# Modulation sums spread over the stages by rates, their loads tied to a value that each stage makes; second expert table turned and the last norm taken token by token

## The chip, the cores and the metric

One NeuronCore of a Trainium2 chip runs the whole program; the other cores are idle. The metric is the device time of one execution in microseconds, as the median of several runs. Five engines work side by side, each through its own list of instructions in order: TensorE (PE, matmuls; its weight loads are shown as PEld), VectorE (DVE), ScalarE (ACT), GpSimd (POOL) and SyncE (SP, which here only issues DMAs). An instruction waits on semaphores for what it needs, and everything behind it on its engine waits with it. A DMA is issued from an engine's list, so an issue that has to wait holds up that engine too.

## What is computed

256 latent tokens and 256 context tokens, 1024 wide, go through two layers (l = 0 works on both, l = 1 on the latents alone), and then the latents through a second block. Cut to what matters:

```python
for l in range(2):                                    # block 1
    ml = split(silu(c) @ w_ada[l] + b_ada[l], 6)      # modulation vectors, latents
    mc = split(silu(c_ctx) @ w_ada[l] + b_ada[l], 6)  # the same for the context (l = 0)
    h = modulate(rmsnorm(x), ml[0], ml[1])
    y = mixer(h)      # 4 mLSTM heads, 8 differential attention heads, Fourier, merged by gates
    x = x + ml[2] * y
    x = x + ml[5] * swiglu(modulate(rmsnorm(x), ml[3], ml[4]))
# block 2: HGRN and S5 mixer, then PEER (128 x 128 = 16384 experts), modulated in the same way
x = x + gt2 * peer(h2)      # sum over experts: gates * gelu(h2 . u_e) * v_e
return rmsnorm(x, final_norm_w)
```

All in float32. A matmul of float32 exactness is made of three fp32r matmuls: high part by high part, high by low, low by high.

## The kernel before

**Tables.** Every weight table comes by DMA as a `raw` tile of 128 x 1024 (512 KB, three buffers). ACT casts it to the high part `whi` (L181, or L201 in the stretches whose order is written out), DVE subtracts to get the low part `wlo` (L186, L202); two buffers each. PE then runs the three products of each table. Activations have hi and lo tiles in the same way (`h`, `hl`, `yb`).

**Background work.** The program is written as a stream of table products; after each one `spend(us)` is called with its estimated time. `spend` advances a clock, and for each `step` of it calls `tick`, which lets the heads started with `go` (mLSTM, attention, Fourier) put their next few small instructions between the products. `spend` also calls `fill` once, which takes the next item of the list `todo`.

**Modulation.** `todo` holds the work on `w_ada`. Part of layer 0's is done on PE at the start (`ada_half`). The rest are 208 sums on DVE (L353, in `ada_sums`): a row tile `ada` of 128 x 1024 is multiplied by the activated conditioning vector `cb`, broadcast over the partitions, and added up along the row. The `ada` tiles are 128 loads of 512 KB into two buffers, issued from SP's queue, which also carries the weight tables. In layer 0 one load serves two sums (64 sums, latents and context); for layer 1 (96) and block 2 (48) it serves one. `ada_rows` makes `cb`: one load of 1 MB (later one of 0.5 MB), a tanh on ACT in pieces (L323) and a product on DVE (L325). Layer 0 needs its remaining vectors by the end of its mixer, layer 1 by its start, and so on.

**Who sets the order.** In the automatic stretches the build's scheduler orders each engine's list by what is ready; there the position in which the code states a sum or a load says little, unless something that the sum needs is made late. After `ordered()` (start and `first_products`, the FFN with `norm_ahead`, PEER) each engine keeps the order that is written.

**End.** `peer_v` walks over the 128 tables of the second expert table in pairs. The gates times activations are kept as hi and lo tiles (`pAh`, `pBl`, 256 tokens). The table is the weight that PE holds and the tokens stream by: 24 matmuls per table of 128 x 256 into four accumulators `ps`, `ps`, `po`, `pada`, with dimensions down the partitions. After the last pair come the residual (L2092), squares (L2094), their sums over partitions by small matmuls (L2084), the root (L416, L417), its spread over the partitions (L425), a copy (L2105), eight products (L2108, L2110) and eight stores (L2111). The output leaves the chip transposed, and the host turns it.

In the profile the functions are found at: `spend` L109, `ada_rows` L313, `ada_load` L328, `ada_sums` L334, the mLSTM heads' chains L772 to L851, attention L879 to L952, `peer_v` L2023.

Of the kernel before, what the change touches and what calls it, by code (L numbers as in the profile page):

```python
# [30 lines left out]
P = 128  # L31
# [8 lines left out]
STEP = [(4.4, 2.8, 3.2), (4.6, 3.3, 2.6)]  # L40
CTX, LAT = slice(0, T), slice(T, T2)
# [8 lines left out]
class K:  # L50
    def __init__(self, tc, d, ctx):
# [6 lines left out]
        self.todo = []  # L58
        self.ahead = []
# [253 lines left out]
    def ada_rows(self, src, ns):  # L313
# [3 lines left out]
        nc.sync.dma_start(cb, bass.AP(tensor=src.tensor, offset=src.offset, ap=[[0, P], [D, ns], [1, D]]))  # L317
# [399 lines left out]
    def ml_qkv(self, l, h, hs, need_ctx, qk):  # L717
# [6 lines left out]
        for i in range(0 if qk else 2):  # L724
            for t, w, c in ((k, "w_mlk", cols), (q, "w_mlq", qc)):
                acc = self.ps("acc")
                self.gemm_t(acc[:, c], d[w][l, 2 * h + i], hs, c)
                nc.scalar.copy(t[:, i, c], acc[:, c])  # L728
        self.tok_major(v, d["w_mlv"][l, h], hs, range(4))
        return q, k, v  # L730

    def tok_major(self, v, src, hs, tts):
# [4 lines left out]
        for i, a in enumerate(accs):  # L737
            nc.scalar.copy(v[:, tts[2 * i]:tts[2 * i] + 2].rearrange("p a b -> p (a b)"), a)

    def ml_o(self, l, h, hs, th):  # L740

        W = self.W
        for i in range(2):
            acc = self.ps("acc")
            self.gemm_t(acc[:, :W], self.d["w_mlo"][l, 2 * h + i], hs, self.hc)
            self.nc.scalar.activation(th[:, i, :W], acc[:, :W], AF.Tanh, scale=0.5)  # L746

# [134 lines left out]
    def da_qk(self, l, h, hs, need_ctx):  # L882
# [9 lines left out]
        nc.scalar.copy(k, acc)  # L892

# [89 lines left out]
    def merge(self, l, b, n, hs, ys, y):  # L983
# [4 lines left out]
        nc.scalar.activation(th[:, :W], acc[:, :W], AF.Tanh, scale=0.5)  # L988
        acc = self.ps("acc")
# [98 lines left out]
    def layer(self, l, x, ada, *begun):  # L1088
# [25 lines left out]
        if l == 0:  # L1114
# [3 lines left out]
            for i, acc in enumerate(accs[1:]):  # L1118
                nc.scalar.copy(qk[(i + 1) % 2][:, i // 2], acc)
        else:  # L1120
# [42 lines left out]
        self.step = STEP[l][0]  # L1163
# [8 lines left out]
        self.step = STEP[l][1]  # L1172
        for h in range(8):
# [5 lines left out]
            if h == 1:  # L1179
                self.drain("ml")  # L1180
                for n in range(KT):
                    self.merge(l, 0, n, hs, ys, y)
        streams_fn = [0, 1] if need_ctx else [1]
        self.step = STEP[l][2]
# [59 lines left out]
        self.ordered()  # L1244
        hs = []
# [777 lines left out]
    def peer_v(self, G, spill, sgs, x, ada, fw, out):  # L2023
# [40 lines left out]
        for j in range(P - 2):  # L2064
# [7 lines left out]
            for n in range(KT):  # L2072
                product(i, e, hi, lo, n, j == 0, False)

        w = [self.wload(d["peer_v"][:, 2 * pairs[63] + e], 8, P) for e in range(2)]
        sq, ss = G[:, 2 * KT:3 * KT], self.ps("t")

        def weighted(n):
            for m in (n - 1, n):
                nc.scalar.activation(G[:, m], x[m], AF.Copy, scale=fw[:, m:m + 1])  # L2080

        def sums(n):
            for j in range(2):
                nc.tensor.matmul(ss[:, j:j + 1], sq[:, n, j * P:(j + 1) * P], c["one1"], start=n == 1 and j == 0,  # L2084
                                 stop=n == KT - 1, skip_group_check=j == 1)

        for n in range(KT):
            for e in range(2):
                product(63, e, *w[e], n, False, e == 1)
            if n % 2:  # L2090
                for m in (n - 1, n):
                    nc.vector.scalar_tensor_tensor(x[m], accs[m // 2][:, (m % 2) * T:(m % 2) * T + T],  # L2092
# [228 lines left out]
```

## Time and profile before

| | |
|---|---|
| median of 3 runs | 3074.4 us (3071.04 to 3077.4) |
| profiled execution | 3075.71 us, of which the traced span is 3073.9 us |
| PE busy | 2961.0 us, 96% of the span |
| DVE busy | 2147.3 us, 70% |
| ACT busy | 1332.0 us, 43% |
| POOL busy | 408.0 us, 13% |
| mean granted TensorE clock | 0.988 of full speed |

The stretches are, by time in the span: start and first products to about 60 us; layer 0's mLSTM heads 60 to 300, attention to 700 (with the first merge, products of w_gp and of the branch table, between heads 1 and 2), last two merges 700 to 850, output product and FFN to 1200; layer 1's heads around 1250 to 1500, attention to 1750, its FFN to about 2000; block 2 to the end, with the two expert tables from about 2300 on. Busy PE means that a matmul stood in the array's pipeline, not that it worked at its peak; idle time of another engine costs nothing unless PE, or the end, waits for it.

### The profile page before, as it was taken

What the parts mean: (1) busy time and instruction counts of PE and PEld (TensorE: products, weight loads), DVE (VectorE), ACT (ScalarE), POOL (GpSimd) and SP (SyncE); (2) the same over time, 40 slices, a digit from 0 to 9 for tenths busy, and PEclk for the clock granted to TensorE, in tenths of its full rate; (3) what the DMA queues carried; (4) which work ended last, traced back from release to release, by engine and by line L of the source; (5) the groups of instructions that cost most, each with busy time, mean ns of one, the idle gap of its engine ahead of it and who ended that gap; (6) DMA issues with size and microseconds to landing.
All of it is one profiled execution on the core that took longest, in us unless ns stands there. A gap on an engine that the chain in (4) does not pass through costs nothing.

```text
span 3073.9 us, 51558 instructions
## 1 busy us (share of the span) xinstructions
PE 2961.0 (96%) x20266; PEld 2680.2 (87%) x20266; DVE 2147.3 (70%) x4042; ACT 1332.0 (43%) x2289; POOL 408.0 (13%) x493
## 2 busy tenths in 40 slices
PE   7999999999999999989999999999899999999998
PEld 5777787888887888878898999987899999999998
DVE  5998637754367555897668667688589878866665
ACT  3333425543243222443446554454445444544444
POOL 2211101101130000321001122770200000000000
PEclk9999999999999999999999999999999999999999
DMA  7555222112333343467442355542457765466664
GB/s 254 178 191 172 70 89 71 67 49 83 100 120 117 132 150 142 152 223 258 142 133 96 111 197 168 179 151 90 134 181 229 231 198 161 154 233 230 224 233 165
DMA packets 151283, 480.90 MB, mean 156 GB/s; under 512 B 19616, under 2 KB 23520, under 8 KB 150912
## 3 DMA queue, kind: packets, MB, share of 16 engines
q1 hardware_dynamic: 145584, 466.39, 46.0%
q0 software_dynamic: 2576, 7.55, 0.9%
q8 instruction: 159, 2.61, 0.4%
q10 hardware_dynamic: 2880, 3.67, 0.3%
q14 instruction: 84, 0.69, 0.1%
HBM read 459.42 MB, written 18.12 MB: 155 GB/s over the span
## 4 chain that ended last, share of the span: by engine, by line
issue 29%; PE 16%; DVE 6%; DMA 2%; ACT 1%; POOL 1%; POOLq 0%; DVEq 0%; ACTq 0%
PE pacc L235 4%; PE pacc L234 4%; PE pacc L233 4%; DMA ada<-in_w_ada_dram 2%; DVE wlo L186 1%; DVE junk L353 1%; PE pacc L231 1%; DVE wlo L202 1%; PE po L845 1%; PE pacc L253 0%; PE pacc L255 0%; PE pacc L254 0%; DVE ropeb L879 0%; POOL ssum L403 0%; DVE hl L506 0%
## 5 line engine op out<-in xcount | busy, mean ns | idle before, releaser
L186 DVE TENSOR_TENSOR wlo<-raw,whi 128x1024 fp32r<-128x1024 f32 x480 | 609.6, 1270 | 352.4 <-ACT whi L181 345.7
L181 ACT CAST whi<-raw 128x1024 fp32r<-128x1024 f32 x480 | 502.7, 1048 | 747.9 <-PE pacc L234 450.9
L233 PE MATMUL pacc<-h,whi 128*128 128x512 f32 (+1 forms) x1280 | 475.1, 371 | 2.0 <-ACT q L728 1.3
L235 PE MATMUL pacc<-h,wlo 128*128 128x512 f32 (+1 forms) x1280 | 467.3, 365 | 5.6 <-DVE wlo L186 5.6
L234 PE MATMUL pacc<-h,whi 128*128 128x512 f32 (+1 forms) x1280 | 467.4, 365 | 3.0 <-DVE h L506 3.0
L233 PE MATMUL pacc<-hl,whi 128*128 128x256 f32 x1504 | 430.1, 286 | 0.2 <-ACT whi L201 0.2
L234 PE MATMUL pacc<-hl,whi 128*128 128x256 f32 x1504 | 425.4, 283 | 4.7 <-DVE hl L506 4.4
L235 PE MATMUL pacc<-hl,wlo 128*128 128x256 f32 x1504 | 425.7, 283 | 3.2 <-DVE wlo L202 1.5
L201 ACT CAST whi<-raw 128x1024 fp32r<-128x1024 f32 (+2 forms) x207 | 189.9, 926 | 375.2 <-PE pacc L234 281.9
L234 PEld LDWEIGHTS pacc<-hl,whi 128*128 128x128 f32 x1504 | 286.4, 190 | 6.5 <-DVE hl L506 6.1
L235 PEld LDWEIGHTS pacc<-hl,wlo 128*128 128x128 f32 x1504 | 285.2, 190 | 4.6 <-DVE wlo L202 2.4
L233 PEld LDWEIGHTS pacc<-hl,whi 128*128 128x128 f32 x1504 | 287.1, 191 | 0.5 <-ACT whi L201 0.4
L235 PEld LDWEIGHTS pacc<-h,wlo 128*128 128x128 f32 x1280 | 243.2, 190 | 48.0 <-DVE wlo L186 7.7
L353 DVE SCALAR_TENSOR_TENSOR junk<-ada,cb 128x1024 bf16<-128x1024 f32 x208 | 258.3, 1242 | 35.7 <-DMA ada<-in_w_ada_dram 34.7
L234 PEld LDWEIGHTS pacc<-h,whi 128*128 128x128 f32 x1280 | 243.6, 190 | 44.0 <-DVE h L506 4.6
L233 PEld LDWEIGHTS pacc<-h,whi 128*128 128x128 f32 x1280 | 243.2, 190 | 44.2 <-ACT q L728 1.5
L202 DVE TENSOR_TENSOR wlo<-raw,whi 128x1024 fp32r<-128x1024 f32 (+2 forms) x163 | 200.2, 1228 | 96.4 <-ACT whi L201 95.7
L235 PE MATMUL pacc<-yb,wlo 128*128 128x512 f32 (+1 forms) x624 | 225.2, 361 | 0.8 <-DVE wlo L186 0.7
L233 PE MATMUL pacc<-yb,whi 128*128 128x512 f32 (+1 forms) x624 | 226.0, 362 | 0.0
L234 PE MATMUL pacc<-yb,whi 128*128 128x512 f32 (+1 forms) x624 | 224.9, 360 | 0.0
L253 PE MATMUL pacc<-whi,h 128*128 128x256 f32 x704 | 202.5, 288 | 3.2 <-ACT oth L746 3.2
L255 PE MATMUL pacc<-wlo,h 128*128 128x256 f32 x704 | 198.9, 283 | 4.9 <-DVE wlo L186 3.3
(587 smaller groups left out, 6480.9 us busy)
## 6 DMA issues: line engine op xcount, KB each, us to landing
ada<-in_w_ada_dram SPq DMA_DIRECT2D x128, 512.0 KB, 3.7
raw<-in_peer_u_dram SPq DMA_DIRECT2D x128, 512.0 KB, 3.8
raw<-in_peer_v_dram SPq DMA_DIRECT2D x128, 512.0 KB, 3.7
raw<-in_w_f_dram SPq DMA_DIRECT2D x120, 512.0 KB, 3.7
raw<-in_w_gp_dram SPq DMA_DIRECT2D x48, 512.0 KB, 3.3
spill<-k SPq DMA_DIRECT2D x61, 256.0 KB, 4.2
k<-spill SPq DMA_DIRECT2D x61, 256.0 KB, 2.6
raw<-in_w_out_dram SPq DMA_DIRECT2D x24, 512.0 KB, 3.3
```

What stands on the lines that cost most here:

```text
L181: nc.scalar.copy(hi, raw)
L186: self.nc.vector.tensor_sub(lo, raw, hi)
L201: self.nc.scalar.copy(hi, raw)
L202: (self.nc.gpsimd if self.spare else self.nc.vector).tensor_sub(lo, raw, hi)
L231: nc.tensor.matmul(acc, hi[:, k], xh[:, cols], start=k == first, stop=(k + 1) % kt == first)
L233: nc.tensor.matmul(acc, hi[:, k], xh[:, cols], start=k == first, stop=False)
L234: nc.tensor.matmul(acc, hi[:, k], xl[:, cols], start=False, stop=False)
L235: nc.tensor.matmul(acc, lo[:, k], xh[:, cols], start=False, stop=(k + 1) % kt == first)
L253: nc.tensor.matmul(a, xh[:, s], hi[:, k], start=half + k == 0 and not sk, stop=False, skip_group_check=sk)
L255: nc.tensor.matmul(a, xh[:, s], lo[:, k], start=False, stop=half * 4 + k == 7, skip_group_check=sk)
L353: nc.vector.scalar_tensor_tensor(self.junk, wt, 0.5, self.cb[:, s], op0=ALU.mult, op1=ALU.mult, accum_out=out[:, s, 8 * r + j:8 * r + j + 1])
L845: nc.tensor.matmul(po[:, :w], aT[:, s * P:(s + 1) * P], vof(s), start=s == 0, stop=s == nk // P - 1)
```

## The change

1. `spend` no longer takes one item of `todo` per product. It adds `us * rate` to `owed` and takes an item for each whole unit. `RATE` gives a rate for each layer and stage: heads, attention, the first merge, and the rest with the FFN.
2. The loads of `ada` and `cb` are issued from ACT's queue instead of SP's, and each is preceded by a copy on ACT of one element (`behind`) of a tile that the current stage has just made (`recent`) into the tile to be loaded. The load then can't come before that value is there. In the FFN `recent` is None and the order is the written one.
3. `wait`, the number of idle items before layer 0's first sums, goes from 4 to 1.
4. `peer_v` is turned: the gate tiles (128 tokens of `pAh` or `pBl`) are the weights that PE holds, and the table streams by in rows of 512, so that a table takes 12 matmuls of 128 x 512 and the accumulators have tokens down the partitions. Residual, gate vector and norm weight are brought to that form ahead (16 transposes of `x` on PE with 4 copies on ACT; four loads that spread a row over the partitions). The last two pairs are held to the end and run accumulator by accumulator, their parts in `pAh`/`whi` and `hl` tiles. Each accumulator's squares are summed along the row by ACT's accumulator, and the root, scaling and store (four of 256 KB) follow by token block.

```diff
+RATE = [(0.12, 0.03, 0.28, 0.30), (0.1, 0.1, 0.2, 0.0)]
...
     def spend(self, us):
-        self.fill()
+        self.owed += us * self.rate
+        while self.owed >= 1.0:
+            self.owed -= 1.0
+            self.fill()
...
         cb = self.t([P, 2, D], "cb", 1)[:, :ns]
-        nc.sync.dma_start(cb, bass.AP(tensor=src.tensor, offset=src.offset, ap=[[0, P], [D, ns], [1, D]]))
+        self.behind(cb[:, 0])
+        nc.scalar.dma_start(cb, bass.AP(tensor=src.tensor, offset=src.offset, ap=[[0, P], [D, ns], [1, D]]))
...
+    def behind(self, t):
+
+        if self.recent is not None:
+            self.nc.scalar.copy(t[0:1, 0:1], self.recent)
+
     def ada_load(self):
         if self.ada_src:
             wt = self.t([P, D], "ada", 2)
-            self.nc.sync.dma_start(wt, self.ada_src.pop(0))
+            self.behind(wt)
+            self.nc.scalar.dma_start(wt, self.ada_src.pop(0))
...
                 nc.scalar.copy(t[:, i, c], acc[:, c])
+                self.recent = t[0:1, i, c][:, 0:1]
...
-        self.step = STEP[l][0]
+        self.step, self.rate = STEP[l][0], RATE[l][0]
...
         self.ordered()
+        self.recent, self.rate = None, RATE[l][3]
...
-        def product(i, e, hi, lo, n, f, l):
-            wh, wl = ws[i]
-            o = accs[n // 2][:, (n % 2) * T:(n % 2) * T + T]
-
-            nc.tensor.matmul(o, hi[:, n], wh[:, e], start=f and n % 2 == 0, stop=False, skip_group_check=n % 2 == 1)
-            nc.tensor.matmul(o, hi[:, n], wl[:, e], start=False, stop=False, skip_group_check=n % 2 == 1)
-            nc.tensor.matmul(o, lo[:, n], wh[:, e], start=False, stop=l, skip_group_check=n % 2 == 1)
+        def product(i, e, hi, lo, a, f, l):
+
+            wh, wl = (w[:, e, a // 2 * P:a // 2 * P + P] for w in ws[i])
+            vh, vl = (v[a % 2] if isinstance(v, list) else v[:, a % 2 * 4:a % 2 * 4 + 4].rearrange("p a b -> p (a b)")
+                      for v in (hi, lo))
+            nc.tensor.matmul(accs[a], wh, vh, start=f, stop=False)
+            nc.tensor.matmul(accs[a], wl, vh, start=False, stop=False)
+            nc.tensor.matmul(accs[a], wh, vl, start=False, stop=l)
...
+        def transposed(a):
+            pt = self.ps("acc")
+            for j in range(4):
+                nc.tensor.transpose(pt[:, j * P:(j + 1) * P], x[a % 2 * 4 + j][:, a // 2 * P:a // 2 * P + P], c["ident"])
+            xt.append(take())
+            late.append((xt[-1], pt))
...
+        for a in range(4):
+            for i in (62, 63):
+                for e in range(2):
+                    product(i, e, *w[i, e], a, False, (i, e) == (63, 1))
+            x0, y = take(), take()
+            nc.vector.tensor_mul(x0, accs[a], gt[a % 2])
+            nc.vector.tensor_add(x0, x0, xt[a])
+            nc.scalar.activation(junk, x0, AF.Square, scale=1.0 / 32, accum_out=ss[:, a:a + 1])
+            nc.vector.tensor_mul(y, x0, fwr[a % 2])
+            ys.append(y)
+            if a % 2:
+                col = ss[:, 4 + a:5 + a]
+                nc.vector.scalar_tensor_tensor(col, ss[:, a - 1:a], 1e-6, ss[:, a:a + 1], op0=ALU.add, op1=ALU.add)
+                nc.gpsimd.tensor_tensor(rs[:, a:a + 1], col, c["mhalf"][:, 0:1], op=ALU.pow)
+                r = rs[:, a:a + 1]
+                nc.scalar.activation(ys[a - 1], ys[a - 1], AF.Copy, scale=r)
+                nc.scalar.dma_start(out[a // 2][:, 0:T2], ys[a - 1])
+                nc.vector.tensor_scalar(ys[a], ys[a], r, None, op0=ALU.mult)
+                nc.sync.dma_start(out[a // 2][:, T2:D], ys[a])
```

What the build makes of it is seen in the engines' lists. In ACT's list at the start of the program, where `h` are the high parts of the first normed activations (each serves `first_products` on PE), before:

```order
L201 CAST whi_414<-raw_259 128x1024
L504 ACTIVATE h_441<-k_105_438,ada_14_104 128x256 x2
L504 ACTIVATE h_450<-k_108_447,ada_14_104 128x256 x2
L201 CAST whi_456<-raw_306 128x1024
L504 ACTIVATE h_463<-k_113_460,ada_14_104 128x256 x2
L504 ACTIVATE h_472<-k_116_469,ada_14_104 128x256 x2
```

and now:

```order
L208 CAST whi_414<-raw_259 128x1024
L345 DMA ada_436<-in_w_ada_dram 128x1024
L345 DMA ada_438<-in_w_ada_dram 128x1024
L325 DMA cb_440<-in_c_rows_dram 128x2048
L518 ACTIVATE h_447<-k_108_444,ada_14_104 128x256 x2
L331 ACTIVATE pada_865<-cb_440 128x512
L518 ACTIVATE h_456<-k_111_453,ada_14_104 128x256 x2
L208 CAST whi_462<-raw_306 128x1024
L331 ACTIVATE pada_971<-cb_440 128x512
L518 ACTIVATE h_469<-k_116_466,ada_14_104 128x256 x2
```

Three loads and the tanh of `cb` (L331) now stand between the casts and the `h` of the first products; of the loads, that of `cb` waits for the semaphore that the first `ada` load signals when it has landed.

In DVE's list in layer 0's mLSTM heads, before, where `den` and `e` are a head's own chain and `junk` is a modulation sum:

```order
L353 SCALAR_TENSOR_TENSOR junk_101,ada_14_104<-ada_1820,cb_796 128x1024
L804 TENSOR_SCALAR e_192_917<-e_192_917,den_194_924 128x256
L796 TENSOR_TENSOR den_206_981<-den_206_981,gc_870 128x2
L186 TENSOR_TENSOR wlo_1072<-raw_1068,whi_1070 128x1024
L805 SCALAR_TENSOR_TENSOR e_192_917<-e_191_916,den_194_924,e_192_917 128x128
L797 RECIPROCAL den_206_981<-den_206_981 128x2
L353 SCALAR_TENSOR_TENSOR junk_101,ada_14_104<-ada_1916,cb_796 128x1024
L799 TENSOR_SCALAR e_196_933<-e_196_933,den_206_981 128x256
```

and now, around the same table:

```order
L812 SCALAR_TENSOR_TENSOR den_206_981<-den_978 128x2
L813 TENSOR_TENSOR den_206_981<-den_206_981,gc_872 128x2
L814 RECIPROCAL den_206_981<-den_206_981 128x2
L816 TENSOR_SCALAR e_196_933<-e_196_933,den_206_981 128x256
L817 SCALAR_TENSOR_TENSOR e_196_933<-e_197_934,den_206_981,e_196_933 128x128
L193 TENSOR_TENSOR wlo_1072<-raw_1068,whi_1070 128x1024
```

The sums between the links of the chain are gone from this place. By their place in the list between the same products, the 208 sums stood before 8 up to 100 us, 86 in 100 to 300, 66 in 925 to 1300 and 48 in 1300 to 1500; now they stand 4 up to 100, 10 in 100 to 300, 24 in 300 to 475, 21 in 575 to 700, 33 in 700 to 850, 87 in 925 to 1300, 10 in 1325 to 1500 and 19 in 1500 to 1750 (on the time scale of the kernel before).

Where they went is seen, for one, in DVE's list in layer 0's first merge (L1011 adds a merged product to the sum `x`), now:

```order
L193 TENSOR_TENSOR wlo_3427<-raw_3423,whi_3425 128x1024
L367 SCALAR_TENSOR_TENSOR junk_101,ada_14_104<-ada_3416,cb_440 128x1024
L1011 SCALAR_TENSOR_TENSOR x_2331<-k_677_3383,pacc_3385 128x512
L367 SCALAR_TENSOR_TENSOR junk_101,ada_14_104<-ada_3416,cb_440 128x1024
L193 TENSOR_TENSOR wlo_3464<-raw_3460,whi_3462 128x1024
L367 SCALAR_TENSOR_TENSOR junk_101,ada_14_104<-ada_3453,cb_440 128x1024 x2
L193 TENSOR_TENSOR wlo_3501<-raw_3497,whi_3499 128x1024
```

Before, the low parts `wlo` of the tables followed each other there with no sum between them.

## Rows read from the trace of the kernel before

**Rows 1.** The page: busy time by engine, and the chain by engine.

```profile
PE 2961.0 (96%) x20266; PEld 2680.2 (87%) x20266; DVE 2147.3 (70%) x4042; ACT 1332.0 (43%) x2289; POOL 408.0 (13%) x493
...
issue 29%; PE 16%; DVE 6%; DMA 2%; ACT 1%; POOL 1%; POOLq 0%; DVEq 0%; ACTq 0%
```

**Rows 2.** Windows: length, busy PE, PEld, DVE, ACT, POOL; PEclk, DMA share, GB/s.

```profile
100.00:300.00 200.00, 184.60 (x948) 151.18 (x947) 179.04 (x389) 73.44 (x155) 35.87 (x33) 0.97 0.59 189
300.00:400.00 100.00, 95.53 (x480) 77.78 (x480) 65.08 (x141) 46.43 (x102) 11.92 (x16) 1.00 0.19 64
700.00:850.00 150.00, 150.00 (x665) 122.33 (x664) 61.95 (x59) 40.16 (x52) 17.96 (x16) 1.00 0.27 91
950.00:1200.00 250.00, 250.00 (x1080) 202.64 (x1079) 145.93 (x214) 62.09 (x74) 0.00 (x0) 1.00 0.38 138
1300.00:1500.00 200.00, 178.09 (x1146) 156.65 (x1145) 159.07 (x299) 78.61 (x150) 31.61 (x34) 0.97 0.68 223
2700.00:3000.00 300.00, 300.00 (x2503) 300.00 (x2502) 190.50 (x209) 136.48 (x157) 0.00 (x0) 1.00 0.68 229
```

**Rows 3.** Windows of line 353 alone: DVE busy (sums and accumulator reads together).

```profile
100.00:300.00 200.00, 106.95 (x172) 0.97 0.59 189
1300.00:1500.00 200.00, 59.02 (x96) 0.97 0.68 223
```

**Rows 4.** Line 353: ns min/median/max, and DVE's idle time before it.

```profile
L353 DVE SCALAR_TENSOR_TENSOR junk<-ada,cb x208: 1197/1219/2320, 74.5 to 1484.7; 128x1024 bf16<-128x1024 f32 x104
...
  DMA ada<-in_w_ada_dram: 34.7, 26
```

**Rows 5.** PE's waits between 100 and 300 us: total us, times, longest.

```profile
PE pt L836 <- DVE den L797: 2.0, 1, 2.0
```

**Rows 6.** PE's waits between 1300 and 1500 us.

```profile
PE pacc L235 <- DVE wlo L186: 4.5, 3, 2.9
```

**Rows 7.** PE's waits between 300 and 400 us.

```profile
PE po L845 <- DVE hn L851: 1.9, 3, 1.0
```

**Rows 8.** Timeline of ACT at the start: start, duration, idle before.

```profile
43.84 1.05 ACT L201 CAST whi<-raw 128x1024 fp32r<-128x1024 f32 x1 [8.04 <-PE ps L472]
...
49.93 0.91 ACT L504 ACTIVATE h<-k,ada 128x256 fp32r<-128x256 f32 x2 [1.01 <-DVE k L491]
...
70.92 0.60 ACT L323 ACTIVATE pada<-cb 128x512 f32<-128x512 f32 x1 [1.52 <-DMA cb<-in_c_rows_dram]
```

**Rows 9.** Timeline of PE at the start.

```profile
54.96 0.50 PE L472 MATMUL pacc<-h,whi 128*128 128x512 f32 x1 [1.71 <-DVE h L506]
```

**Rows 10.** DMA issues: count, KB each, median us from issue to landing.

```profile
ada<-in_w_ada_dram SPq DMA_DIRECT2D x128, 512.0 KB, 3.7
...
cb<-in_c_rows_dram SPq DMA_DIRECT2D x1, 1024.0 KB, 8.6
...
out_dram<-G ACTq DMA_DIRECT2D x4, 128.0 KB, 2.0
```

**Rows 11.** Single operations from groups by line, and one of PE's timeline.

```profile
L2111 ACTq DMA_DIRECT2D out_dram<-G x4: 345/412/467, 3068.5 to 3070.0; - x4
...
L847 ACT ACTIVATION_READ_ACCUMULATOR hn<-po x72: 188/195/224, 124.7 to 1730.4; 128x1 f32 x72
...
155.85 0.60 PE L818 MATMUL pt<-c_ident,hn 128*128 128x128 f32 x4
...
L2048 DVE TENSOR_TENSOR pBl<-k,pAh 128x512 fp32r<-128x512 f32 x9 | 6.2, 685 | 0.0
```

**Rows 12.** Timeline of the end, from the last pair of tables.

```profile
3056.41 0.39 PE L2057 MATMUL ps<-pAh,wlo 128*128 128x256 f32 x1 [0.76 <-DVE wlo L186]
...
3061.54 0.28 PE L2057 MATMUL pada<-pAh,wlo 128*128 128x256 f32 x1
...
3065.61 0.70 POOL L417 TENSOR_TENSOR col<-col,c_mhalf 128x2 f32<-128x2 f32 x1 [841.45 <-DVE col L416]
...
3068.82 1.82 SPq L2111 DMA_DIRECT2D out_dram<-G  x4
```

More of the change, by code (lines that the diff above doesn't have):

```diff
@@ L58, in __init__ @@
         self.todo = []
+        self.rate, self.owed, self.recent = 0.0, 0.0, None
         self.ahead = []
@@ L1119, in layer @@
                 nc.scalar.copy(qk[(i + 1) % 2][:, i // 2], acc)
+            self.recent = qk[0][0:1, 1, 0:1]
         else:
@@ L1171, in layer @@
         y = [self.t([P, W], "x" if need_ctx else "xl", KT) for _ in range(KT)]
-        self.step = STEP[l][1]
+        self.step, self.rate = STEP[l][1], RATE[l][1]
         for h in range(8):
@@ L1180, in layer @@
                 self.drain("ml")
+                self.rate = RATE[l][2]
                 for n in range(KT):
                     self.merge(l, 0, n, hs, ys, y)
+                self.rate = RATE[l][1]
         streams_fn = [0, 1] if need_ctx else [1]
-        self.step = STEP[l][2]
+        self.step, self.rate = STEP[l][2], RATE[l][2]
         fo = []
@@ L2063, in peer_v @@
         load(3)
-        for j in range(P - 2):
+        for j in range(P - 4):
             i, e = j // 2, j % 2
@@ L2071, in peer_v @@
                 load(i + 4)
[L2072 to L2092, printed above, removed]
-                                                   ada[:, 0, 40 + m:41 + m], x[m], op0=ALU.mult, op1=ALU.add)
-                    nc.scalar.activation(sq[:, m], x[m], AF.Square)
-                if n > 2:
-                    nc.vector.tensor_add(sq[:, n - 2], sq[:, n - 3], sq[:, n - 2])
-                    weighted(n - 2)
@@ L2098, in peer_v @@
-        for n in (1, 3, 5, 6, 7):
-            sums(n)
-        weighted(KT - 1)
-        rs = self.t([P, 8], "col8", 2)
-        self.rstd(rs[:, :2], ss[:, :2])
-        pr = self.rows(rs, 2, "acc")
-        r = G[:, 3 * KT]
-        nc.scalar.copy(r, pr[:, :T])
-        for m in (0, 5, 1, 2, 6, 3, 4, 7):
-            if m < 5:
-                nc.vector.tensor_mul(G[:, KT + m], G[:, m], pr[:, :T])
-            else:
-                nc.gpsimd.tensor_tensor(G[:, KT + m], G[:, m], r, op=ALU.mult)
-            (nc.sync if m % 2 else nc.scalar).dma_start(out[m], G[:, KT + m])
+            for a in range(4):
+                product(i, e, hi, lo, a, j == 0, False)
@@ new lines, in peer_v @@
+            if j in side:
+                side[j]()
+            elif late and j % 4 == 2:
+                nc.scalar.copy(*late.pop())
+        gated(63)
+        w = {(62, e): self.wload(d["peer_v"][:, 2 * pairs[62] + e], 8, P) for e in range(2)}
+        parts(63)
+        for e in range(2):
+            raw = self.t([P, KT, P], "raw", 3)
+            nc.sync.dma_start(raw, d["peer_v"][:, 2 * pairs[63] + e])
+            w[63, e] = [], []
+            for half in range(2):
+                r = raw[:, 4 * half:4 * half + 4].rearrange("p (a c) b -> p a (c b)", a=2)
+                hi, lo = (self.t([P, 2, T + 2], "hl", KT, F32R)[:, :, :T] for _ in range(2))
+                nc.scalar.copy(hi, r)
+                nc.vector.tensor_sub(lo, r, hi)
+                w[63, e][0].append(hi)
+                w[63, e][1].append(lo)
@@ new lines, in peer_v @@
+        ss = self.t([P, 8], "col8", 2)
+        rs = self.t([P, 8], "rs8", 2)
+        junk, ys = take(), []
+        for a in range(4):
+            for i in (62, 63):
+                for e in range(2):
+                    product(i, e, *w[i, e], a, False, (i, e) == (63, 1))
[14 more added lines that the diff above has]
+                nc.sync.dma_start(out[a // 2][:, T2:D], ys[a])
@@ L2148, in rounds @@
                 rows = d["c_rows"][l:] if (l, r) in ((0, 2), (2, 0)) else None
-                k.todo.append(k.ada_sums(rows, r, bt, out, ns, 4 if (l, r) == (0, 2) else 0))
+                k.todo.append(k.ada_sums(rows, r, bt, out, ns, 1 if (l, r) == (0, 2) else 0))
     rounds(0, 2, d["ada_b"][0])
```

21 lines of the change are left out of this document (19 added, 2 removed).

## The prediction, made before the changed kernel had run

> **What bounds the kernel now.** I began with the page. PE is busy 96% of the span, DVE 70%, ACT 43%, and the chain that ended last is mostly PE and PE's issue, with 6% on DVE and 2% on DMA [rows 1]. So PE bounds the kernel, and a change is worth what it takes from PE's work, from PE's idle time or from the tail behind the last product. The windows then say where PE is idle. In layer 0's mLSTM heads (100 to 300 us) it idles 200 − 184.6 = 15.4 us, in layer 1's (1300 to 1500) 21.9 us, and in both the granted clock is 0.97, a mean that holds some time at the lower level (1.2 instead of 2.4 GHz), against 1.00 in the other windows; in the last two merges, the FFN and the second expert table PE has no idle time at all [rows 2]. In layer 0's heads DVE is busy 179 of 200 us, and 107 of these are the modulation sums, 86 of them (172 counts, each sum with an accumulator read); in layer 1's heads 59 us are 48 sums [rows 3]. A sum is 1.22 us long, and DVE stood idle 34.7 us in all before sums whose load hadn't landed [rows 4]: what stands behind such a sum in DVE's list waits too. The list of waits shows who that is: PE stood for a head's `den` [rows 5] and for low parts of tables [rows 6]. In 300 to 400 us, where no sum stands but the heads still run, PE idles 4.5 of 100 us at clock 1.00 [rows 2], and its waits there are for a head's own `hn` [rows 7]. That is my yardstick for heads without sums: 9.0 us in 200.
>
> I make the sum against the profiled execution, 3075.7 us; the median of the runs is 1.3 below it.
>
> **Sums taken out of the heads.** Layer 0: idle 15.4, and a clock of 0.97 costs another 0.03 × 200 = 6.0, together 21.4; less the yardstick 9.0 leaves 12.4 for 86 sums, 0.14 each. The change takes 76 of them away: −11. Layer 1: 21.9 + 6.0 − 9.0 = 18.9 for 48 sums, 0.39 each (each has a load of its own there); 38 go: −15. Bounds: no more than a third of it, if the idle time is mostly the heads' own (−9 for both), and all idle and clock loss of both windows, 21.4 + 27.9 = 49, if the yardstick is too high.
>
> **Sums put elsewhere.** 118 sums appear where none stood. The 33 in the last merges meet a PE that never waits and a DVE busy 62 of 150 us [rows 2]: 33 × 1.3 = 43 us more still fit, 0. The 45 in layer 0's attention and first merge I price between 0 and the 0.14 above: +3. The FFN gets 21 more beside 66; its DVE has 104 of 250 us free and PE hides it: I add 2 (0 to 4) for layer 1's loads, of which each serves one sum only. The 19 in layer 1's attention lie between 0.14 and 0.39 each, 2.7 to 7.4: +4. Together +9.
>
> **Loads on ACT.** 128 loads now cost ACT an issue of 0.41 us each and a copy of one element, for which the nearest row is the small accumulator read of 0.20 [rows 11]: 78 us in all on an engine that is busy 20 to 45% of these windows [rows 2]. The cover is ACT's free time; what waits behind a blocked load are the casts `whi`, then PE. I put 0 here, except at the start. SP's queue loses these issues and gains the four spreads; PE waits for no issue of SP's where it has no idle time, and I give that nothing either.
>
> **The start.** ACT's list now has the loads of two `ada` tiles and of `cb`, then one `h`, then the tanh of `cb`, then the next `h`. The `cb` load waits for the first `ada` load to land, 3.7 us [rows 10] after its issue behind the cast that ends at 44.9 [rows 8], so it goes out near 49; it took 8.6 us to land before [rows 10]. The tanh, which before ran at 70.9 behind everything, then stands until about 57.5 and takes 0.6, and the `h` that started at 49.93 [rows 8] starts near 58: 8 us late. PE needs it for the first products. A stall of 1.7 us there [rows 9] falls inside the new one, and four sums now stand before the tables' low parts: +1. I take +7. Bounds: +3, if the 1 MB lands in half the time while little else is loaded, and +14, if PE also comes back at the lower clock level, as it does in the heads.
>
> **The turned table.** 24 × 128 = 3072 matmuls of 256 columns become 1536 of 512. A narrow one takes 300 / 2503 = 119.9 ns in this very stage; a wide one, in the FFN where PE never waits either, 250 / 1080 = 231.5 ns [rows 2]. Two narrow ones are 239.7, so each pair saves 8.2 ns: −12.6 us. The 16 transposes cost 0.15 each, as four took 0.60 [rows 11]: +2.4. The four copies on ACT (half as wide as the cast of 1.05 [rows 8], so 0.5 each) lie beside 300 − 136 free us of ACT per 300; the four spreads and their loads lie under 60 tables of products. The bounds are 0, if the wide ones here keep the narrow ones' rate, and −12.6.
> A rule to be weighed here speaks against this size. The Trainium skill, "TensorE: Matmul & The Clock Gate", section "Back-to-back issue gap", gives an isolated matmul columns / 2.4 + 2.5 ns. By that a pair would save only 2.5 ns, an estimate of 3.8 us in all, and the total would come out 9 us higher. The rows stand at 119.9 and 231.5, both above what the formula gives (109.2 and 215.8), and I go by them.
>
> **The tail.** Before, the last product ended at 3061.8 and the last store left the queue at 3070.6, then 3.3 us to the end of the span [rows 12]: 8.8 + 3.3. Now, after the last accumulator, there is a product and an add of 0.69 each [rows 11], a square with its accumulator read (0.8), a tiny add (0.16), the power of 0.70 [rows 12], a scaling (0.6, half the cast's width again), an issue (0.4) and hand-offs (0.5): 4.6. The store is 256 KB and not 128, which landed in 2.0 [rows 10]: +0.5. That gives −3.7. The last two pairs need four tables' parts before their first product ends, where before PE stood 0.8 us for a low part [rows 12]; I add 0.9 for more of the same. Together −2.8.
>
> **The sum.** −11 − 15 + 9 + 7 − 12.6 + 2.4 − 2.8 = −23.0. 3075.7 − 23.0 = 3052.7, and 1.3 less on the median: **3051 us**.
>
> **Rivals.**
> *The heads are freed altogether.* The yardstick of 9 us in 200 is taken from a stretch that also holds attention. If the mLSTM heads by themselves leave PE no idle time and the clock stays at 1.00, 49 us go instead of 26, for 3028. For it: DVE would fall from 179 to about 85 of 200 us [rows 2, 3]. Against it: the waits for `hn` where no sum stands [rows 7].
> *The heads keep their stalls.* The chain `den`, `e`, `hn` may be as long without sums, since its links wait for PE and ACT too. With a third of the 26 saved the time is 3051 + 17 = 3068.
> *The added sums stall PE (slower).* A sum that stands before a low part in DVE's list, and whose load is held back by `behind`, stops PE wherever it is put. Without the added sums' 9 the sum is −32, so at 32 / 118 = 0.27 us for each of the 118 the gain is gone; at layer 1's present price of 0.39 it is +46 − 32 = +14, which gives 3088. Against it: most of these places have a PE without idle time and a DVE less than 60% busy [rows 2].
> *The wide matmuls don't save what the rows promise.* The narrow ones' 119.9 is from a stage with a DMA share of 0.68, the wide ones' 231.5 from one with 0.38 [rows 2]; if the difference is the stage's and not the width's, the saving lies between 0 and half, and the time is 3057 to 3064, say 3060. The skill's formula above gives 3060 as well.
> *The start is worse*, +14 in place of +7: 3058.
>
> **Chances.** Forecast 0.45 (its own range 3040 to 3062), heads freed 0.17, heads keep their stalls 0.13, narrow saving 0.10, worse start 0.08, added sums stall 0.07. A measurement of this kernel can tell about 0.2%, 6 us: faster is below 3068.3, slower above 3080.5. Half of the third case falls within: faster 0.85, same 0.08, slower 0.07. The range runs from 3028 to 3068: outside it lie about 0.06 of the freed heads, 0.06 of the kept stalls and 0.07 of the stalling sums.
>
> **What would show it.** Heads: in the first 300 us and again in layer 1's heads PE's idle time near 9 per 200 us with a clock of 1.00, and no `den` or low part at the head of PE's waits. Start: the tanh of `cb` between two `h` and PE idle some 7 us before the product that follows. Turn: about 231 ns per matmul in the last 700 us. Tail: some 8.5 us from the last product to the end of the span. Merges, FFN and attention: PE's idle time as before, with the sums now there. I am wrong if the stages that received the sums show new waits for low parts, if a blocked load on ACT holds up casts later than the start, or if the heads' idle time stays.

## The result and the profile after

The changed kernel takes 3024.76 us in the median (3022.9 to 3027.75, four runs) against 3075.23 (3071.04 to 3077.4): a ratio of 0.9841, 95% interval 0.9825 to 0.9857. It is 50 us faster where I had forecast 24; 3025 lies 3 us below the low end of my range and beside the rival "the heads are freed altogether" (3028).

The page of the kernel after, engines in the order of [rows 1]:

```profile
PE 2928.8 (97%) x18722; PEld 2589.2 (86%) x18722; DVE 2152.6 (71%) x4043; ACT 1344.9 (44%) x2362; POOL 401.9 (13%) x492
```

DVE does as much as before; PE has 1544 instructions fewer and a higher share of a shorter span. The windows of the kernel after, columns as in [rows 2]; stages start some 17 us earlier from 300 us on:

```profile
100.00:300.00 200.00, 199.70 (x1070) 166.97 (x1069) 99.63 (x238) 81.59 (x174) 24.20 (x34) 1.00 0.31 95
300.00:400.00 100.00, 96.31 (x462) 77.78 (x461) 77.77 (x159) 45.79 (x103) 10.67 (x11) 1.00 0.34 116
700.00:850.00 150.00, 149.87 (x646) 121.23 (x645) 104.40 (x129) 47.13 (x75) 27.61 (x25) 1.00 0.52 168
950.00:1200.00 250.00, 250.00 (x1079) 202.62 (x1079) 170.86 (x258) 62.68 (x77) 0.00 (x0) 1.00 0.53 163
1300.00:1500.00 200.00, 196.37 (x1305) 175.03 (x1304) 134.30 (x246) 94.59 (x186) 27.15 (x34) 0.99 0.50 154
2700.00:3000.00 300.00, 299.19 (x1325) 246.72 (x1324) 198.33 (x218) 145.01 (x168) 0.00 (x0) 1.00 0.72 241
```

Read the first row against its counterpart in [rows 2]: in layer 0's heads PE idles 0.3 us where it idled 15.4, the granted clock is 1.00 where it was 0.97, and DVE has fallen from 179 to 100 of 200 us. The second row still has its 4 us of idle time. That is the stretch from which I took my yardstick, so this alone shows that its idle time says nothing of the 200 us before it. The trace of the kernel before has the reason, which I had overlooked. PE's two longest waits between 300 and 400 us there, and one of an mLSTM head:

```profile
308.09 1.99 PE L845 MATMUL po<-v,aT 128*128 128x256 f32 x8 [0.30 <-DVE hn L851]
344.19 0.39 PE L927 MATMUL ps<-k,oth 128*128 128x256 f32 x1 [1.77 <-ACT e L932]
361.44 1.13 PE L845 MATMUL po<-v,aT 128*128 128x128 f32 x8 [1.04 <-DVE hn L851]
```

Lines L836 to L851 belong to a helper that the mLSTM heads and attention share. An mLSTM head's `po` is 256 wide, attention's 128. The last `po` of an mLSTM head starts at 315.6; what waits behind it for `hn` is attention, and so is the 1.77 for `e`. An mLSTM head's own wait in this stretch is 0.30 us.

To see where the time went I laid the traces side by side by work that all kernels share: the low parts `wlo` of the tables come in the same order everywhere, so the start of the n-th one dates the same place in each. The table gives, stage by stage, how many us a kernel needs more (+) or less (−) than the one before, each from one profiled execution (spans 3024.6 and 3073.9 for the first row). The experiments further down are in it too. A column ends at the low part nearest to the time under its name; attn0+ takes in the merges.

```
stage (us before)  start  heads0  attn0+   FFN0  heads1  attn1  block 2  table2    end    all
                    to 60  to 306  to 949 to 1276 to 1515 to 1740 to 2707 to 3049
after                 4.1   -22.5     3.1   -0.7   -26.1    8.4      4.0   -15.4   -4.2  -49.3
e1_turn              -0.4    -1.8     0.0   -0.4     1.5    0.0     -2.3   -15.8   -4.3  -23.6
e2_rates              4.2   -23.3     5.9   -1.2   -25.1    6.3     -1.8    -0.0   -0.4  -35.4
e3_sums_alone         0.9    -3.6     2.1   -2.3    -9.9    0.1      0.3     0.0   -0.6  -13.0
e4_loads_alone        0.4    -9.4     2.2   -2.6   -17.2    0.0     -0.5     0.0   -1.2  -28.2
e6_none               0.2   -23.5     0.2   -2.9   -28.1    0.0     -0.4     0.0   -1.0  -55.3
e11_traffic           0.6   -20.4     0.4   -2.9   -16.9   -0.0      0.9    -0.0    0.0  -38.3
e9_unheld             5.0    -3.4     3.0   -0.8   -14.2    0.0      2.7   -14.5   -4.6  -26.7
e10_heads             3.6   -15.6     4.9   -5.1   -26.5    0.0     -0.4   -14.8   -4.7  -58.7
e7_ffn                2.5   -22.6     4.6    8.0   -27.6    0.0      2.7   -15.8   -4.6  -52.7
e8_start             -0.1   -23.6     3.4   -0.5   -27.0    7.5      1.1   -14.7   -4.6  -58.5
e12_small             2.9   -22.6     3.3   -3.6   -27.1    3.4      0.6   -14.1   -4.6  -61.9
e13_best             -0.0   -23.1     7.8   -5.0   -27.3    0.2      2.1   -14.5   -4.6  -64.4
```

Two stages make the gain, 49 us in the heads; a third, the second table, 15; layer 1's attention gives 8 back. Block 2's +4.0 before its tables lies, for 3.4 of it, where the granted clock was lower than in the kernel before. Its longest part, one and the same run of matmuls in every kernel, in the kernel before, the kernel after and e2_rates:

```profile
2068.27:2178.41 110.14, 101.15 (x1073) 85.81 (x1071) 82.92 (x142) 47.37 (x99) 4.28 (x14) 0.98 0.28 87
```
```profile
2035.27:2147.66 112.39, 102.78 (x1073) 86.89 (x1071) 82.94 (x142) 47.60 (x99) 4.26 (x14) 0.97 0.29 86
```
```profile
2034.13:2142.11 107.98, 99.56 (x1072) 84.58 (x1071) 82.92 (x143) 47.35 (x99) 4.25 (x14) 1.00 0.26 89
```

The same work took 112.4 us at a mean clock of 0.97, 110.1 at 0.98 and 108.0 at 1.00. Nothing of the change stands there, so I count such differences of up to 4 us as chance of one execution.

### The profile page after: what moved, and what is told of

It reads as the page before. It is cut to its first block, busy times and chain, and to the rows that moved or that the text cites. A ratio compares the mean times of both kernels' runs of the same rounds, so it can differ in the third digit from the quotient of the medians.

```text
span 3024.6 us, 48489 instructions
## 1 busy us (share of the span) xinstructions
PE 2928.8 (97%) x18722; PEld 2589.2 (86%) x18722; DVE 2152.6 (71%) x4043; ACT 1344.9 (44%) x2362; POOL 401.9 (13%) x492
## 4 chain that ended last, share of the span: by engine, by line
PE 55%; DVE 8%; DMA 2%; ACT 2%; issue 2%; POOL 1%; SPq 0%; ACTq 0%; POOLq 0%; DVEq 0%
PE pacc L242 12%; PE pacc L241 12%; PE pacc L240 12%; PE ps L2036 2%; PE ps L2081 2%; PE ps L2079 2%; PE ps L2080 2%; DVE wlo L193 1%; PE pacc L262 1%; PE pacc L260 1%; PE pacc L261 1%; PE po L2079 1%; PE po L2080 1%; PE pada L2080 1%; PE pada L2079 1%
## 5 line engine op out<-in xcount | busy, mean ns | idle before, releaser
L193 DVE TENSOR_TENSOR wlo<-raw,whi 128x1024 fp32r<-128x1024 f32 x478 | 597.6, 1250 | 330.5 <-ACT whi L188 319.9
L367 DVE SCALAR_TENSOR_TENSOR junk<-ada,cb 128x1024 bf16<-128x1024 f32 x208 | 265.8, 1278 | 81.3 <-DMA ada<-in_w_ada_dram 78.6
```

What stands on the lines that cost most here:

```text
L193: self.nc.vector.tensor_sub(lo, raw, hi)
L367: nc.vector.scalar_tensor_tensor(self.junk, wt, 0.5, self.cb[:, s], op0=ALU.mult, op1=ALU.mult, accum_out=out[:, s, 8 * r + j:8 * r + j + 1])
```

## The experiments

**One part at a time.** e1_turn has part 4 alone, e2_rates parts 1 to 3 alone; their edits are those parts of the diff above, for instance

```diff
e1_turn:
-            nc.tensor.matmul(o, hi[:, n], wh[:, e], start=f and n % 2 == 0, stop=False, skip_group_check=n % 2 == 1)
+            nc.tensor.matmul(accs[a], wh, vh, start=f, stop=False)
e2_rates:
-        self.fill()
+        self.owed += us * self.rate
```

> The kernel before with part 4 of the change alone (turned second expert table and the last norm by tokens; sums and loads as before). My forecast gave this part -12.6 + 2.4 - 2.8 = -13 us, so 3062. The aligned traces of before and after show -16 over the table and -4 behind it: if that is the part's own doing, -20 and 3055. The rival that the turn only gains because the stages ahead changed (other buffers, other DMA traffic) gives something between 3062 and 3075.

> The kernel before with parts 1 to 3 alone (rates, loads held by a value, wait 1; the table and the end as before). My forecast gave these -11 - 15 + 9 + 7 = -10 us, so 3065. The aligned traces show about -29: +4 at the start, -22 and -26 in the two stretches of heads, +8 in layer 1's attention, the rest small and, in block 2, +5 that no part explains. If the parts are independent: 3046. If the +5 in block 2 is chance: 3041.

e1_turn: 3059.84 us, ratio 0.9963 (0.9949 to 0.9976). e2_rates: 3041.22, ratio 0.9901 (0.9886 to 0.9917). As medians the parts give −12 and −30 against 3071.66, and their profiled executions −23.6 and −35.4; e1's runs spread from 3052 to 3063, as those of the kernel before do by some 10 us, so that its median says less than the place of its gain. The table shows the parts independent: what e1 gains lies in the second table and the end, what e2 gains in the heads, and each stage comes out as in the full change. The kernel after has 3024.76 and e2 3041.22, so the turn and its end are worth some 16 us beside the new rates (18 by the two ratios, 20 by the two stages of the table).

**What in the heads stalled PE.** Four kernels made from the one before take the sums apart. e3_sums_alone keeps the sums and drops the loads, e4_loads_alone keeps the loads and shrinks the sums, e11_traffic keeps the loads and has no sums, e6_none has neither.

```diff
e3_sums_alone (e6_none too, without the sum):
-            self.nc.sync.dma_start(wt, self.ada_src.pop(0))
+            if len(self.ada_kept) < 2:
+                self.nc.sync.dma_start(wt, src)
e4_loads_alone:
-                nc.vector.scalar_tensor_tensor(self.junk, wt, 0.5, self.cb[:, s], op0=ALU.mult, op1=ALU.mult,
+                nc.vector.scalar_tensor_tensor(self.junk[:, :8], wt[:, :8], 0.5, self.cb[:, s, :8], op0=ALU.mult, op1=ALU.mult,
e11_traffic, e6_none:
-                nc.vector.scalar_tensor_tensor(self.junk, wt, 0.5, self.cb[:, s], op0=ALU.mult, op1=ALU.mult,
-                                               accum_out=out[:, s, 8 * r + j:8 * r + j + 1])
```

> The kernel before, all sums in their old places, but only the first two row tiles are loaded; all 208 sums read these two, so the sums are of the wrong rows. It tells what in the heads stalled PE. If it is DVE's time for the sums (1.3 us each between the links of a head's chain), little changes: 3070 or more, PE still idle some 15 and 20 us in the two windows of heads. If it is the waiting for loads, or the traffic that they add (DMA share 0.59 and 0.68 there), the heads come free and the time falls by 30 to 45 us, to 3030 to 3045.

> The kernel before, all 128 loads, but each sum takes 8 of its 1024 columns, so that the sums are of a part of a row. The counterpart: if DVE's time is the cause, the heads come free, 3030 to 3045; if the loads are, the time stays at 3065 or more. My forecast's yardstick (9 us of idle time per 200 us of heads that are their own) would give -26 at most, 3049.

> The kernel before without the 208 sums and without all but two of their loads (the modulation is set to zero, so the tokens go through unmodulated). It gives the bound for the heads. My forecast's yardstick says that heads without sums keep 9 us of idle time per 200 us: -12 and -19 against before, 3041. If the heads have hardly any stalls of their own: -22 and -26 or somewhat more, 3022 to 3026, and PE is busy at least 198 of 200 us in the first window.

> The kernel before with all 128 loads and no sum at all (modulation zero). With the loads and sums of 8 columns 14 and 11 us of the heads' 23 and 28 stayed. If these were the loads' traffic (DMA share 0.6 beside the tables), they stay here: 3046 to 3052. If they were DVE standing at a sum whose load hadn't landed, with the chains and low parts queued behind it, they go: 3022 to 3027.

| kernel | us | ratio (95%) |
|---|---|---|
| e3_sums_alone | 3059.48 | 0.9956 (0.994 to 0.9971) |
| e4_loads_alone | 3050.36 | 0.9935 (0.9919 to 0.995) |
| e11_traffic | 3034.45 | 0.9875 (0.986 to 0.989) |
| e6_none | 3022.6 | 0.984 (0.9825 to 0.9855) |

Windows of e6_none in both layers' heads, and just behind layer 0's:

```profile
100.00:280.00 180.00, 180.00 (x974) 150.86 (x973) 80.34 (x206) 72.32 (x151) 19.29 (x30) 1.00 0.26 82
290.00:390.00 100.00, 95.56 (x460) 77.16 (x459) 61.78 (x126) 44.98 (x96) 10.49 (x13) 1.00 0.20 69
...
1290.00:1470.00 180.00, 177.31 (x1169) 157.16 (x1168) 103.54 (x188) 79.33 (x147) 28.46 (x34) 1.00 0.36 116
```

Without sums layer 0's heads keep no idle time at all: the whole 23.5 us was owed to the sums and their loads. Layer 1's keep 2.7 of 180 us, at clock 1.00. The 4.4 us in the row behind layer 0's heads stay, as in every kernel (4.0 to 6.3 in the same stretch of work). This is where my yardstick failed.

The window of layer 0's heads in e3_sums_alone:

```profile
100.00:300.00 200.00, 186.46 (x972) 153.10 (x971) 185.28 (x404) 73.80 (x155) 37.74 (x33) 0.97 0.23 77
```

The loads are gone (DMA share 0.23 instead of 0.59), but DVE is 93% busy, and PE idles 13.5 us at clock 0.97. In layer 0 DVE's time for the sums is enough by itself for 20 of the 23.5 us. The loads with hardly any sum cost PE much too, in another way. DVE's waits between 100 and 300 us in e4_loads_alone, and in the kernel before:

```profile
DVE junk L353 <- DMA ada<-in_w_ada_dram: 39.6, 28, 4.0
```
```profile
DVE junk L353 <- DMA ada<-in_w_ada_dram: 6.0, 8, 1.1
```

A sum of 8 columns takes 0.25 us with its accumulator read instead of 1.3, yet DVE stands 39.6 us in front of 28 of them, up to 4.0 us each, until their loads land, with the heads' chains queued behind; 14 us stay. In e11_traffic, where no sum stands in DVE's list, 3 stay: so the traffic itself costs little in layer 0, and 11 us are the standing with the 80 small sums. But this standing is e4's more than the kernel before's: there DVE, kept at work by the full sums, stood 6.0 us before 8 of them. So in layer 0's heads the main cause before the change is DVE's own time for the sums.

In layer 1 it is not settled. e11_traffic and e4_loads_alone gain the same 17 of 28 us, so 11 stay with the loads in either. The longest of PE's waits in e11_traffic between 1290 and 1470 us:

```profile
PE pacc L233 <- ACT whi L181: 4.1, 1, 4.1
```

PE waits for the high part of a table there, not for a chain. But ACT, which makes it, had just been held by the issues of eight stores, `park`; their row in e11_traffic, and in the kernel before:

```profile
L1151 ACTq DMA_DIRECT2D park<-x x8: 326/350/1306, 1294.1 to 1302.6; - x8
```
```profile
L1152 ACTq DMA_DIRECT2D park<-x x8: 336/466/516, 1318.0 to 1321.5; - x8
```

From the first issue to the last it took 8.5 us in e11, where no sum paces the loads and they come packed, and 3.5 in the kernel before. So 4 of the 11 us come from a stall that the kernel before doesn't have, and how much the loads' traffic cost layer 1's heads there stays open. e11_traffic's 3034 fell between my two expectations: the heads of layer 0 came free, those of layer 1 did not. The costs of layer 0 overlap (20, 14 and 3 of 23.5), so they can't be added.

**Whether the tie is needed, and what a tied sum costs.** e9_unheld is the changed kernel without the copy, e10_heads the changed kernel with more sums in the heads.

```diff
e9_unheld:
-            self.nc.scalar.copy(t[0:1, 0:1], self.recent)
+            pass
e10_heads:
-RATE = [(0.12, 0.03, 0.28, 0.30), (0.1, 0.1, 0.2, 0.0)]
+RATE = [(0.43, 0.03, 0.28, 0.30), (0.3, 0.1, 0.2, 0.0)]
```

> The changed kernel without the copy that ties each load to a value; rates and queue stay. In the build's lists the sums are then back in the heads (88 of 208 between 50 and 300 us, 27 of them after 1300). If their place is what counts, the gain of the heads is gone and the turned table's stays: 3050 to 3062. If the rates or ACT's queue make the gain: 3025.

> The changed kernel with a higher rate in the heads, sums still tied: some 58 instead of 14 in layer 0's heads, none left after 1250 us, so that layer 1's heads and attention are free of them. Price by the number of sums (22 us for 76 taken out, 0.3 each): +13 in layer 0's heads, -12 in layer 1, 3026. If the price came from the crowding (loads that land after their sum's turn) and not from the number: about 0 in layer 0's heads and -12 in layer 1, 3013.

e9_unheld: 3044.07, ratio 0.9907 (0.9892 to 0.9922). e10_heads: 3017.02, ratio 0.9823 (0.981 to 0.9837). In e9 the build's order puts the sums back, and the table shows −3.4 in layer 0's heads where the tied kernel has −22.5. The rates and ACT's queue alone do nothing there: without a value to wait for, the scheduler takes each sum as early as it can. (In layer 1 only 27 sums come back instead of 48, so half of that gain stays and the time is a little below what I expected.) Windows of layer 0's heads in e9 and in e10:

```profile
100.00:280.00 180.00, 167.50 (x864) 137.66 (x862) 164.26 (x349) 66.11 (x138) 29.91 (x33) 0.99 0.60 189
```
```profile
100.00:280.00 180.00, 175.69 (x923) 145.58 (x922) 135.24 (x299) 74.07 (x168) 22.60 (x29) 0.99 0.48 157
```

PE idles 12.5 us with DVE at 164 of 180, 4.3 with DVE at 135, and next to nothing with DVE at 80 to 106 (e6_none, e13_best). Against e6_none the stretch from 60 to 306 us costs 1.0 us with the change's 13 sums, 7.9 with e10's 55, 20.1 with e9's 91 and 23.5 with before's 94: 0.08, 0.14, 0.22 and 0.25 us per sum. The price of a sum is not a constant; it rises as DVE fills. e10 is 8 us faster than the change all the same: by the table it loses 6.9 us in layer 0's heads and gains 8.4 in layer 1's attention, then free of sums, and 4.4 in the FFN, which has fewer; the 4.4 in block 2 are in the order of chance.

**Layer 1's attention.** e7_ffn moves all remaining sums to layer 0's FFN; e12_small keeps every load and copy and shrinks block 2's sums, 29 of which stand in layer 1's heads and attention.

```diff
e7_ffn:
+RATE = [(0.12, 0.03, 0.28, 0.42), (0.1, 0.0, 0.2, 0.0)]
e12_small:
+                n = 8 if ns == 1 else D
+                nc.vector.scalar_tensor_tensor(self.junk[:, :n], wt[:, :n], 0.5, self.cb[:, s, :n], op0=ALU.mult, op1=ALU.mult,
```

> The changed kernel with layer 0's FFN at a rate of 0.42 instead of 0.30: all sums are then done before layer 1's heads. If the 8 us that layer 1's attention lost and the rest of its heads' stalls come from the sums and loads there: -8 to -12, 3013 to 3017. If the FFN pays for them in turn (DVE would be busy some 230 of 250 us there) or the 8 us are the copies' and the order's: 3022 to 3030.

> The changed kernel with block 2's 48 sums taken over 8 of 1024 columns, their loads and copies kept (block 2's modulation is wrong). 29 of them stand in layer 1's heads and attention, where the attention lost 8 us. If DVE's time for the sums is the price: 3016. If the copies and loads on ACT's list are, which hold up ACT's casts and copies there: 3024.

e7_ffn: 3023.03, ratio 0.9842 (0.9829 to 0.9856). e12_small: 3013.89, ratio 0.9815 (0.98 to 0.983). PE's waits in layer 1's attention in the kernel after (1473 to 1706 us):

```profile
PE pt L853 <- DVE dast L948: 2.4, 2, 2.2
PE po L862 <- ACT k L931: 2.1, 1, 2.1
PE po L862 <- ACT aT L855: 1.1, 1, 1.1
PE po L862 <- ACT whi L188: 0.9, 1, 0.9
```

Some name DVE, some ACT. With no sum there the 8.4 us go altogether (e7, e10); with sums of 8 columns 3.4 stay. So 5 are DVE's time for 18 sums. What makes the other 3.4 is not shown: e12 keeps the loads and the copies on ACT, but DVE also stands before late loads there. DVE's row and PE's longest wait in e12_small from 1473 to 1706 us:

```profile
DVE junk L368 <- DMA ada<-in_w_ada_dram: 8.3, 5, 4.1
```
```profile
PE po L863 <- DVE hn L869: 2.9, 1, 2.9
```
In e7 the FFN takes the 8 us back. Its window:

```profile
930.00:1180.00 250.00, 246.41 (x1059) 198.88 (x1060) 198.28 (x309) 62.51 (x76) 0.00 (x0) 1.00 0.65 206
```

DVE was at 171 and PE without idle time in the kernel after; at 198 PE loses 3.6 us in this window and more behind it.

**The start, and a version that uses all this.** e8_start loads the first two row tiles and the first `cb` from SP's queue; e13_best does so too and spreads all sums over layer 0.

```diff
e8_start, e13_best:
-        nc.scalar.dma_start(cb, bass.AP(tensor=src.tensor, offset=src.offset, ap=[[0, P], [D, ns], [1, D]]))
+        (nc.sync if ns == 2 else nc.scalar).dma_start(cb, bass.AP(tensor=src.tensor, offset=src.offset, ap=[[0, P], [D, ns], [1, D]]))
-            self.nc.scalar.dma_start(wt, self.ada_src.pop(0))
+            (self.nc.sync if len(self.ada_src) > 126 else self.nc.scalar).dma_start(wt, self.ada_src.pop(0))
e13_best:
+RATE = [(0.2, 0.04, 0.38, 0.32), (0.1, 0.1, 0.2, 0.0)]
```

> The changed kernel with the first two row tiles and the first cb loaded from SP's queue, as before, the rest unchanged. PE lost some 4 us at the start behind the tanh of cb. If the load's place in ACT's list makes that: 3021, and the fifth low part comes at its old time. If the tanh alone holds ACT whichever queue loads cb, or SP's tables now come later: 3025.

> The changed kernel with the first loads from SP's queue and layer 0's rates at 0.2, 0.04, 0.38 and 0.32, so that all sums are done before layer 1: 24 in layer 0's heads, some 30 in the attention, 76 in the merges, the rest in the FFN. -4 at the start, -8 and -1 in layer 1, +1 in layer 0's heads: 3013. If DVE in the merges has no room for 51 sums in 150 us (62 + 66 = 128 us busy there): 3018 or more.

ACT's timeline at the start of the kernel after:

```profile
45.38 1.05 ACT L208 CAST whi<-raw 128x1024 fp32r<-128x1024 f32 x1 [8.03 <-PE ps L486]
...
48.84 0.33 ACTq L325 DMA_DIRECT2D cb<-in_c_rows_dram  x1
49.55 0.91 ACT L518 ACTIVATE h<-k,ada 128x256 fp32r<-128x256 f32 x2 [3.12 <-DVE k L505]
53.98 0.60 ACT L331 ACTIVATE pada<-cb 128x512 f32<-128x512 f32 x1 [3.52 <-DMA cb<-in_c_rows_dram]
54.52 0.89 ACT L518 ACTIVATE h<-k,ada 128x256 fp32r<-128x256 f32 x2
```

and of e8_start:

```profile
50.37 0.91 ACT L518 ACTIVATE h<-k,ada 128x256 fp32r<-128x256 f32 x2 [0.94 <-DVE k L505]
51.18 1.03 ACT L208 CAST whi<-raw 128x1024 fp32r<-128x1024 f32 x1
52.22 0.91 ACT L518 ACTIVATE h<-k,ada 128x256 fp32r<-128x256 f32 x2
53.03 0.58 ACT L331 ACTIVATE pada<-cb 128x512 f32<-128x512 f32 x1
```

The tanh stood 3.5 us in ACT's list for `cb`, and the second pair of `h` came at 54.5; with the load on SP the build puts the tanh behind the third pair and PE loses nothing: −0.1 in place of +4.1. e8_start: 3018.52, ratio 0.9826 (0.9813 to 0.9839). e13_best: 3007.06, ratio 0.9787 (0.9774 to 0.9801), 18 us below the change. Of the 15 us between the two profiled spans the start has 4, layer 1's attention 8, its heads 1 and the FFN 4, and layer 0's attention and merges take 5 back. Its window of the last two merges:

```profile
680.00:830.00 150.00, 150.00 (x664) 122.22 (x663) 114.88 (x160) 44.43 (x77) 26.85 (x16) 1.00 0.54 174
```

PE still has no idle time there with DVE at 115 of 150 us, so what I feared of this window didn't come; the 5 us are lost before and behind it, 3.8 of them between 300 and 570.

## Why the prediction was wrong, step by step

*Sums out of the heads, −26 forecast, −48.6 measured.* This is the step that failed: "That is my yardstick for heads without sums: 9.0 us in 200." The stretch 300 to 400 that it came from has 4 to 6 us of idle time in every kernel here, with no sum in it or up to 16. I took the `hn` of [rows 7] for an mLSTM head's; it is attention's but for 0.30 us, and attention runs behind the heads. Without sums layer 0's heads have no idle time and layer 1's 2.7 us in 180 (e6_none). So nearly all of the idle time and of the clock's loss was the doing of the sums and their loads, 21.4 and 27.9 by [rows 2], as the first rival had it; e6_none shows it (23.5 and 28.1). The half of my working that read idle time and clock from the windows was right to 2 us.

*Sums put elsewhere, +9 forecast, +10.8 measured.* Attention and merges of layer 0 +3 and +3.1, FFN +2 and −0.7, layer 1's attention +4 and +8.4. The last was mis-sized: 18 sums there cost 0.47 us each, above my upper bound of 0.39; 0.28 are DVE's time for the sum by e12, and the rest is open. One premise was a slip, there and where I described the kernel: I wrote that a load of layer 1 serves one sum; there too it serves two (32 + 48 + 48 = 128 loads), and only block 2's serve one.

*Loads on ACT: 0 forecast.* Rows of the kernel after, for the copy and the issue:

```profile
L345 ACTq DMA_DIRECT2D ada<-in_w_ada_dram x128: 333/334/447, 45.4 to 1690.6; - x128
...
L339 ACT COPY ada<-k x41: 174/191/193, 237.8 to 1534.4; 1x1 f32<-1x1 f32 x41
```

0.33 and 0.19 us where I had 0.41 and 0.20 [rows 11], and only 41 of the 128 loads have a copy, since at the start and in the FFN there is none. In layer 0's heads PE has no idle time beside them; in layer 1's attention they may be part of the 3.4 us that e12 left open.

*The start, +7 forecast, +4.1 measured.* The mechanism was right, the size off: `cb` landed in 5.1 us, where I took the 8.6 of [rows 10], and the second pair of `h` came at 54.5 instead of 58. Of the 4.1 us, 1.5 were lost ahead of these loads: the cast before them starts at 45.38, in the kernel before at 43.84 [rows 8]. Five other kernels with the same start lost 2.5 to 5.0. PE did come back at the lower clock level (a mean of 0.58 granted from 55.47 to 59.55), but so it had in the kernel before (0.50 from 58 to 60).

*The turned table, −10.2 with the transposes forecast, −15.4 measured.* Its window above holds 16 transposes and 1309 wide matmuls: (299.2 − 2.4) / 1309 = 226.7 ns each, where I took the FFN's 231.5. A pair saves 13 ns and not 8.2, which lies outside the bounds that I gave; over the 119 of 128 tables that lie between the table's two marks that is −18.6, with the transposes −16.2, and the missing 0.8 is in the order of PE's waits for low parts there:

```profile
PE ps L2081 <- DVE wlo L193: 1.8, 4, 0.5
```
By the Trainium skill, "TensorE: Matmul & The Clock Gate", section "Back-to-back issue gap", a pair would have saved 2.5 ns, an estimate from its formula for an isolated matmul. Both measured spacings (119.9 and 226.7) lie above its 109.2 and 215.8, and the measurement decides. Why the wide ones run at 227 here and at 231 in the FFN I have not tested.

*The end, −2.8 forecast, −4.2 measured.* The timeline of the end after, in the order of [rows 12]:

```profile
3016.91 0.39 PE L2081 MATMUL pada<-hl,pAh 128*128 128x512 f32 x1
...
3018.85 0.63 ACT L2150 ACTIVATE G<-G 128x512 f32<-128x512 f32 x1 [1.39 <-DVE G L2149]
...
3019.85 0.56 POOL L2156 TENSOR_TENSOR rs<-col,c_mhalf 128x1 f32<-128x1 f32 x1 [5.00 <-DVE col L2155]
...
3021.19 0.35 ACTq L2159 DMA_DIRECT2D out_dram<-G  x1
```

From the last product's end (3017.3) to the last issue's (3021.5) it takes 4.2 us where I had 4.6, and 3.1 more to the span's end, where I had feared 0.5 on top of 3.3.

The sum of the stages as measured is 4.1 − 22.5 − 26.1 + 10.8 + 4.0 − 15.4 − 4.2 = −49.3; of the 26 us by which the forecast missed, 22.6 are the heads.

## What to carry to other kernels

A yardstick for "what stays when this work is gone" should come from the same code without that work, not from the neighbouring stretch; here the whole idle time and clock loss of the windows was right to 2 us. Look which work stands behind a wait before you give it to a stage: a helper's line can serve several. Filler on an engine that serves others is priced by how full that engine is: in the heads PE lost next to nothing with DVE at 50 to 59%, 4 us of 180 at 75% and 12 at 91%. It is priced too by how long the engine stands before filler that isn't there: in e4_loads_alone PE lost 10 us of 200 with DVE at 48%. A rate in the code holds only what something ties down in the build's order, and a load put in a busy engine's list should not be the one that its own next instruction waits for.

## What the runs showed that I had not expected

In layer 0's heads two causes were each enough for most of the loss by themselves: full sums without loads left 20 us, loads with small sums 14, both together only 23.5. Tied loads land later for their sums than before the change: DVE stood 78.6 us in 47 places, where it had stood 34.7 in 26 [rows 4], and the kernel is faster all the same, for 27 of it fall between 685 and 835 us, in the last two merges, where PE has no idle time. The row of the kernel after:

```profile
  DMA ada<-in_w_ada_dram: 78.6, 47
```

Where PE idled 15 and 22 of 200 us, in the heads before, the granted clock was 0.97; in layer 0's heads after, with 0.3 us, it was 1.00. In 300 to 400 us, with 4.5 of 100, it was 1.00 too [rows 2]. The same 1073 matmuls took 108.0 to 112.4 us depending on the clock that one execution was granted, so single profiles differ by some 4 us in stages that no edit touched. In the narrow form the weight loads filled the whole stage (PEld 300 of 300 us [rows 2]), in the wide one 247.
